# Scratch transfers issued by GpSimd, more staging buffers, and modulation sums closed later, in a two-layer hybrid diffusion backbone

## The chip, the cores and the metric

The kernel runs on one core of a Trainium2 chip. A core has a matrix engine (TensorE, PE), a vector engine (VectorE, DVE), a scalar engine (ScalarE, ACT), GpSimd (POOL) and a sync engine (SyncE, SP). Each works through its own list of instructions in order and waits on semaphores where it needs another engine or a transfer. A transfer is issued by an instruction in one of these lists, and is carried out by the 16 DMA engines that the issuers share. The metric is the device time of one execution in microseconds (us); lower is better.

## The reference

One latent sequence of 256 tokens (a grid of 4 rows of 64) and 256 context tokens, model width 2048, two layers, all float32. Layer 0 has a mixer of eight bidirectional gated-DeltaNet heads (GDN) beside eight neighbourhood-attention heads (NA), layer 1 a short gated convolution; each is followed by a SwiGLU feed-forward of hidden width 5632. Every layer is modulated by six vectors computed from the conditioning vector. Cut to what matters here:

```
for l in range(DEPTH):
    sh1, sc1, g1, sh2, sc2, g2 = jnp.split(jax.nn.silu(c) @ ada_w[l] + ada_b[l], 6, axis=-1)
    h = modulate(x_lat, norm_mix[l], sh1, sc1)          # rmsnorm(x, g) * (1 + scale) + shift
    ...
# even mixer, h latent and hc context
ka, va, kb, vb, a, b, qa, qb, za = split_segments(h @ w_in, EVEN_SEGS)   # hc: the first six
ka, va, qa = short_conv_silu([ka, va, qa], conv_w)
o_l = gdn_bidirectional(q_l, k_l, va, g, beta, s_ctx_fin)   # chunks of 64, both directions
y_gdn = rmsnorm(o_l, gdn_norm) * silu(za)
# attention: window keys of the grid plus all context keys in one softmax
s_loc = q @ k_window * scale + bias_from(rpb);  s_ctx = q @ k_ctx * scale
y_na = softmax(concat(s_loc, s_ctx)) @ concat(v_window, v_ctx)
y = concat(y_gdn, y_na) @ w_out
# GDN, per chunk: T = inverse(I + strictly_lower(beta * k k^T * decay)), then a scan over chunks
```

## The kernel before, in words

**Projections.** Every large product is done as three matmuls: weights and activations are each split into a high and a low part (whi, wlo and so on). A weight tile raw (128x1024, 512 KB) is loaded by SP; ACT copies it to whi (L169), DVE subtracts to get wlo (L238), PE runs hi by hi, lo by hi and hi by lo into PSUM (L284, L285, L287, and L293 to L295 in the last step, and L309 to L313 where the output has features on the partitions). An evacuation function then empties each PSUM tile mm.

**The even mixer**, some 200 to 900 us into the span, is a chain of such streams over column blocks of the input projection: keys KA and values VA of GDN, gates, queries QA, then QB, KB, VB of the attention heads and the gate ZA, then the output projection. The evacuations of QB, KB and VB (`stage`) copy a PSUM tile into a staging tile nst (two buffers), by turns on ACT (L164) and DVE (L166), and store it to DRAM scratch qb_d, kb_d, vb_d (L1051, issued by ACT). ZA uses the same tiles for its store to zd.

**Beside the streams** runs the GDN work. Keys and values go through DRAM scratch too: kd, vd_ and qTd are stored when a head's projection is done; `chunk_matrices` reloads ktok (L776), transposes it to kT and stores that (kTd, L795); it builds the strictly lower blocks n64, n32, stores them (nd64, nd32) and brings the 32x32 diagonal blocks through DRAM (dl, L825, back as lsol) into a layout in which POOL's memset and DVE's 31 steps solve all of them at once (zsol). The result goes out as dz (L846), and `inverses` reloads n64, n32 and the blocks (xd<-dz, xdT<-dz) and completes the inverse with small matmuls (Y, L887). Then scan steps (L927 to L960) run, one chunk after the other. Each reload waits for its store.

**Neighbourhood attention** (`na_scores`, `na_values`) runs head by head: load kb, qb, the relative bias br (one buffer, two issues of ACT at L1081), bq = br + band mask (DVE, L1084), scores (L1088, L1089), softmax, transposes (L188), reload of vb and the values (L1112).

**The modulation sums** (`ada_job`) stream the 512x or 1024-wide blocks of the modulation weights (araw) in 16 steps through DVE, acc = acc + araw * c (L332), into an acc that POOL zeroed (L327) and into whose first row SP loaded the bias (L328). A block then closes: PE sums over partitions (L338). A `Pump` takes such steps at a rate among the steps of the streams.

**What sets the order.** The program is handed to a scheduler that lays out every engine's list by its own simulated times. So an edit at one place can move instructions everywhere. Where two instructions of one engine compete, the list decides, and an instruction that waits holds everything behind it in its list.

**Counters of transfers.** A transfer signals one of a few counters. Those issued by SP and ACT share eight of them, listed as DMAHW0 to DMAHW7 in the engines' lists below; those issued by POOL have others, DMASW0 to DMASW7. An issue that takes a counter waits until the transfer that had it before is through.

Of the kernel before, what the change touches and what calls it, by code (L numbers as in the profile page):

```python
# [41 lines left out]
NPT = 1  # L42
AB = 3
# [4 lines left out]
NST = 2  # L48
# [57 lines left out]
def body(tc, x, c, ctx, c_ctx, ada_w, ada_b, norm_mix, norm_ffn, ffn_w_gate, ffn_w_up, ffn_w_down,  # L106
# [212 lines left out]

    def ada_job(pool_, l, seg, kind, gamma=None, width=1024, bufs=2):  # L320

        wr = ada_w[l].rearrange("(k p) n -> p k n", p=128)
        nf = width // 128
        for blk in range(D // width):
            c0 = seg * D + blk * width
            acc = pool_.tile([128, width], F32, name="acc", tag="acc", bufs=1)
            POOL.memset(acc, 0.0)  # L327
            SP.dma_start(acc[0:1, :], ada_b[l:l + 1, c0:c0 + width])  # L328
            for k in range(KT):
                raw = pool_.tile([128, width], F32, name="araw", tag="araw", bufs=bufs)  # L330
                SP.dma_start(raw, wr[:, k, c0:c0 + width])
                DVE.scalar_tensor_tensor(acc, raw, cT[:, k:k + 1], acc, op0=OP.mult, op1=OP.add)  # L332
                yield
            fs_ = slice(blk * nf, (blk + 1) * nf)
            p = smt()
            if width < 1024:
                for f in range(nf):
                    PE.matmul(p[:, f:f + 1], acc[:, f * 128:(f + 1) * 128], ones[:, 0:1], start=True, stop=True)  # L338
                pc = p
            else:  # L340
                ah = pool_.tile([128, width], F32R, name="ah", tag="ah", bufs=1)
                al = pool_.tile([128, width], F32R, name="al", tag="al", bufs=1)
                split(ah, al, acc, DVE)
                for f in range(nf):
                    for a in (ah, al):
                        PE.matmul(p[0:nf, 0:128], pick[:, nf - 1 - f:2 * nf - 1 - f], a[:, f * 128:(f + 1) * 128],
                                  start=f == 0 and a is ah, stop=f == nf - 1 and a is al)
                g = pool_.tile([16, 128], F32, name="grow", tag="grow", bufs=1)[0:nf]
                acopy(g, p[0:nf, 0:128])
                if kind == "row":  # L350
                    ACT.dma_start(row_d[l, seg][fs_], g)
                    continue
# [6 lines left out]
        if kind == "row" and width < 1024:  # L359
            p = smt()  # L360
            transpose(p[0:16, 0:128], gcol[l, seg])
            g = pool_.tile([16, 128], F32, name="grow", tag="grow", bufs=1)
            DVE.tensor_copy(g, p[0:16, 0:128])
            SP.dma_start(row_d[l, seg], g)
# [7 lines left out]
    class Pump:  # L372
        def __init__(self, jobs, steps, total):
            self.it = (s for j in jobs for s in j)
            self.rate = total / max(steps, 1)
            self.due = 0.0
            self.done = False
# [246 lines left out]
    def ka_evac(q):  # L624
        def done(kt, ss):
            normalise(kt, 4, rstd(kvp, ss, [128, 4, 4], 16, 1.0, "rk"))
            ACT.dma_start(hslice(kd, 0, 4, q), kt.rearrange("p t h e -> p t (h e)"))
        return head_evac(4, q, 0, done, True)

    def va_evac(q):  # L630
        def done(vt, ss):
            ACT.dma_start(hslice(vd_, 0, 4, q), vt.rearrange("p t h e -> p t (h e)"))
        return head_evac(4, q, 8, done, False)

    def qa_evac(q):
        def done(qt, ss):
# [3 lines left out]
            for g in range(2):  # L640
# [6 lines left out]
                ACT.dma_start(qTd[:, q * 4 + g * 2:q * 4 + g * 2 + 2, :], qf)  # L647
# [126 lines left out]
    def load_tok(tag, d_, t0, q):  # L774
        t = g4(tag, tag).rearrange("p (t h e) -> p t h e", t=2, h=4)
        SP.dma_start(t.rearrange("p t h e -> p t (h e)"), hslice(d_, t0, 2, q))  # L776
        return t

    def load_feat(tag, src, pool_=None, bufs=1):
        t = (pool_ or gw).tile([128, 1024], F32, name=tag, tag=tag, bufs=bufs).rearrange("p (h t) -> p h t", h=4)  # L780
        SP.dma_start(t, src)
        return t

    def chunk_matrices(seq):
# [6 lines left out]
        for q in range(2):  # L791
# [3 lines left out]
            SP.dma_start(kTd[:, seq, q * 4:q * 4 + 4, :], kT)  # L795
# [26 lines left out]
        ACT.dma_start(nd64, n64)  # L822
        ACT.dma_start(nd32, n32)
# [19 lines left out]
        for d in range(2):  # L843
            for v in range(2):
                src = (zsol, lsol)[d ^ v][d * 64:(d + 1) * 64].rearrange("p r c -> p (r c)")
                (SP, ACT)[v].dma_start(dz[v, :, :, d].rearrange("b q t e -> (b q) t e"), src)  # L846
        return nd64, nd32, dz

    def inverses(parts, q):
# [4 lines left out]
        SP.dma_start(n64, nd64[:, q * 8:q * 8 + 8, :])  # L854
        SP.dma_start(n32, nd32[:, q * 8:q * 8 + 8, :])
# [187 lines left out]
    def stage(dst, n, by=None):  # L1043

        def f(i, *p):
# [5 lines left out]
            ACT.dma_start(dst(i), st_)  # L1051
# [21 lines left out]
    def na_scores(h):  # L1073
        kb = nap.tile([128, 512], F32, name="kb", tag="kb", bufs=2)
        qb = nap.tile([128, 256], F32, name="qb", tag="qb", bufs=2)
        bq = nap.tile([128, 6, 64], F32, name="bq", tag="bq", bufs=2)
        br = nap.tile([128, 6, 64], F32, name="br", tag="br", bufs=1)
        for half in range(2):
            src = bass.AP(tensor=ev_rpb.tensor, offset=ev_rpb.offset + h * 465 + (5 - half) * 31 + 15 - 63,
                          ap=[[1, 64], [31, 6], [1, 64]])  # L1080
            ACT.dma_start(br[half * 64:half * 64 + 64], src)  # L1081
        SP.dma_start(kb, kb_d[:, h, :])
        SP.dma_start(qb, qb_d[:, h, :])
        DVE.tensor_tensor(bq, br, bandf[:, None, :].to_broadcast([128, 6, 64]), op=OP.add)  # L1084
# [16 lines left out]
    def na_values(h, ss):  # L1101
        vb = nap.tile([128, 4, 128], F32, name="vb", tag="vb", bufs=2)
# [13 lines left out]
    def za_evac(ti, n, p):  # L1116
# [4 lines left out]
        ACT.dma_start(zd[:, ti, n * 512:(n + 1) * 512], o)  # L1121
# [282 lines left out]
```

## Time and profile before

| | |
|---|---|
| median of 3 timed runs | 2842.87 us (2839.62 to 2844.02) |
| the profiled execution, its own time | 2848.17 us |
| its span | 2846.4 us |
| PE busy | 2732.5 us (96%) |
| DVE, ACT, POOL busy | 1924.8 (68%), 1308.3 (46%), 51.1 us (2%) |
| DMA queues | SP's 652.48 MB, ACT's 25.73 MB; none of POOL's |

A row of a view of groups gives the line, the engine, the operation, the tile written and those read, the shape, the count, the busy time, the mean of one in ns, and the idle time of the engine just before with what ended it ("<- DVE nst L166": released by DVE's instruction on nst at line 166). A row of the waits gives the total, the count and the longest. A row of the timeline gives the start, the duration, and in brackets the idle time before it. PEclk is the clock granted to PE as a share of full speed.

### The profile page before, as it was taken

Reading aid. Unit: us, or ns where it says so; the run is one execution under the profiler, and the core shown is the slowest. Engines: PE = TensorE matmul, PEld = TensorE weight load, DVE = VectorE, ACT = ScalarE, POOL = GpSimd, SP = SyncE. Lnnn points to the kernel's source line nnn. Section 1 sums busy time; section 2 is a strip of 40 time slices with the busy share of each in tenths; the row PEclk is TensorE's granted clock in tenths of the full one; section 3 lists DMA queues with packets and bytes.
Section 4 is the critical chain, followed back from the end, with each engine's and each line's share of the span. In section 5 each row is a group of like instructions: output and inputs, shape, how many; then the busy total and the mean of one; then the engine's idle time right before and its main releaser. Section 6 shows DMA issues by size and latency. Waiting matters only on the chain.

```text
span 2846.4 us, 40363 instructions
## 1 busy us (share of the span) xinstructions
PE 2732.5 (96%) x15113; PEld 2281.6 (80%) x15113; DVE 1924.8 (68%) x2647; ACT 1308.3 (46%) x1945; POOL 51.1 (2%) x77
## 2 busy tenths in 40 slices
PE   5999999989989999999999999999999999999998
PEld 3699989888767778888888878878878888888886
DVE  3387767857667878776677768897678644445665
ACT  3267543222354544444445545444454444444554
POOL 0000001000000000000000000000000000000000
PEclk9999999999999999999999999999999999999999
DMA  9955568777758599987788657998559766656653
GB/s 345 311 177 164 143 208 253 243 225 236 210 170 278 200 318 346 347 285 249 272 305 282 198 175 243 328 319 306 179 179 332 262 188 180 195 186 215 192 192 126
DMA packets 284927, 680.78 MB, mean 239 GB/s; under 512 B 57273, under 2 KB 97313, under 8 KB 283323
## 3 DMA queue, kind: packets, MB, share of 16 engines
q1 hardware_dynamic: 262148, 652.48, 69.4%
q10 hardware_dynamic: 22583, 25.73, 3.0%
q8 instruction: 118, 1.93, 0.3%
q14 instruction: 78, 0.64, 0.1%
HBM read 657.63 MB, written 20.48 MB: 238 GB/s over the span
## 4 chain that ended last, share of the span: by engine, by line
PE 70%; DMA 15%; DVE 9%; issue 3%; ACT 2%; SPq 1%; POOL 0%; ACTq 0%; DVEq 0%; POOLq 0%
PE mm L287 17%; PE mm L285 17%; PE mm L284 17%; DMA araw<-in_ada_w_dram 11%; PE mm L313 7%; DVE acc L332 3%; DVE wlo L238 3%; PE sm L188 2%; PE mm L293 2%; PE mm L295 2%; PE mm L294 2%; DMA raw<-in_od_w_in_dram 1%; DMA acc<-in_ada_b_dram 1%; PE gd L477 1%; ACT whi L169 0%
## 5 line engine op out<-in xcount | busy, mean ns | idle before, releaser
L238 DVE TENSOR_TENSOR wlo<-raw,whi 128x1024 fp32r<-128x1024 f32 x800 | 971.5, 1222 | 452.3 <-ACT whi L169 446.3
L169 ACT ACTIVATE whi<-raw 128x1024 fp32r<-128x1024 f32 x800 | 841.9, 1058 | 875.5 <-PE mm L287 632.4
L332 DVE SCALAR_TENSOR_TENSOR acc<-araw,cT,acc 128x1024 f32<-128x1024 f32 (+1 forms) x416 | 431.2, 1037 | 228.4 <-DMA araw<-in_ada_w_dram 198.8
L285 PE MATMUL mm<-wlo,fhi 128*128 128x512 f32 x1232 | 473.6, 394 | 0.2 <-DVE wlo L238 0.2
L284 PE MATMUL mm<-whi,fhi 128*128 128x512 f32 x1232 | 470.9, 396 | 0.6 <-ACT fhi L1187 0.6
L287 PE MATMUL mm<-whi,flo 128*128 128x512 f32 x1232 | 392.2, 392 | 0.1
L284 PEld LDWEIGHTS mm<-whi,fhi 128*128 128x128 f32 x1232 | 232.4, 189 | 50.4 <-ACT fhi L1187 1.0
L287 PEld LDWEIGHTS mm<-whi,flo 128*128 128x128 f32 x1232 | 231.0, 188 | 50.7 <-DVE flo L1189 0.3
L285 PEld LDWEIGHTS mm<-wlo,fhi 128*128 128x128 f32 x1232 | 232.5, 189 | 48.7 <-DVE wlo L238 0.7
L284 PE MATMUL mm<-whi,ahi 128*128 128x512 f32 x672 | 259.8, 392 | 0.0
L285 PE MATMUL mm<-wlo,ahi 128*128 128x512 f32 x672 | 259.4, 391 | 0.0
L287 PE MATMUL mm<-whi,alo 128*128 128x512 f32 x672 | 209.7, 392 | 0.0
L313 PE MATMUL mm<-hllo,whi 128*128 128x256 f32 x640 | 181.1, 287 | 0.0
L313 PE MATMUL mm<-hlhi,wlo 128*128 128x256 f32 x600 | 169.4, 288 | 2.0 <-issue 1.5
L313 PE MATMUL mm<-hlhi,whi 128*128 128x256 f32 x600 | 167.5, 290 | 1.0 <-DVE hlhi L502 1.0
L172 ACT ACTIVATE ahi<-prodT 128x256 fp32r<-128x256 f32 x176 | 73.0, 417 | 194.7 <-PE mm L285 187.6
L285 PEld LDWEIGHTS mm<-wlo,ahi 128*128 128x128 f32 x672 | 126.2, 188 | 27.5
L284 PEld LDWEIGHTS mm<-whi,ahi 128*128 128x128 f32 x672 | 126.2, 188 | 27.2
L287 PEld LDWEIGHTS mm<-whi,alo 128*128 128x128 f32 x672 | 126.1, 188 | 27.3
L285 PE MATMUL mm<-wlo,dhi 128*128 128x512 f32 x336 | 127.3, 398 | 2.6 <-DVE wlo L238 2.4
L313 PEld LDWEIGHTS mm<-hllo,whi 128*128 128x128 f32 x640 | 124.0, 194 | 0.4
L284 PE MATMUL mm<-whi,dhi 128*128 128x512 f32 x336 | 123.5, 396 | 0.3 <-DVE u_t L1329 0.3
(399 smaller groups left out, 4055.9 us busy)
## 6 DMA issues: line engine op xcount, KB each, us to landing
araw<-in_ada_w_dram SPq DMA_DIRECT2D x288, 512.0 KB
raw<-in_ffn_w_down_dram SPq DMA_DIRECT2D x176, 512.0 KB
raw<-in_ffn_w_gate_dram SPq DMA_DIRECT2D x160, 512.0 KB
raw<-in_ffn_w_up_dram SPq DMA_DIRECT2D x160, 512.0 KB
raw<-in_ev_w_in_dram SPq DMA_DIRECT2D x112, 512.0 KB
araw<-in_ada_w_dram SPq DMA_DIRECT2D x192, 256.0 KB
raw<-in_od_w_in_dram SPq DMA_DIRECT2D x96, 512.0 KB
raw<-in_ev_w_out_dram SPq DMA_DIRECT2D x32, 512.0 KB
```

The lines of the kernel that those rows point to most:

```text
L169: ACT.activation(dst, src, AF.Copy)
L172: ACT.activation(hi, src, AF.Copy)
L188: return PE.transpose(dst, src, ident[:n, :n])
L238: DVE.tensor_tensor(lo, raw, hi, op=OP.subtract)
L284: PE.matmul(ps[ti][n], a, hi[:, n * 512:(n + 1) * 512], start=first, stop=False)
L285: PE.matmul(ps[ti][n], a, lo[:, n * 512:(n + 1) * 512], start=False, stop=False)
L287: PE.matmul(ps[ti][n], b, hi[:, n * 512:(n + 1) * 512], start=False, stop=False)
L293: PE.matmul(ps[ti][n], lh(t), hi[:, c_], start=False, stop=False)
L294: PE.matmul(ps[ti][n], lh(t), lo[:, c_], start=False, stop=False)
L295: PE.matmul(ps[ti][n], ll(t), hi[:, c_], start=False, stop=hi is group[-1][0])
L313: PE.matmul(ps[f][:, n * 256:(n + 1) * 256], wt, mv(w, k), start=False, stop=i == len(ks) - 1 and g == len(group) - 1 and j == 2 and w == ...
L332: DVE.scalar_tensor_tensor(acc, raw, cT[:, k:k + 1], acc, op0=OP.mult, op1=OP.add)
```

## The change

Three things change, and two of them through the tile sizes of the same code.

1. POOL issues 86 transfers that ACT or SP issued: the stores kd, vd_, qTd, kTd, nd64, nd32, dl, dz, zd and the 24 of the staging tile, and the reloads of ktok, vtok, kT, qT, n64 and n32. The reloads of lsol that ACT issued go to SP; xd<-dz and xdT<-dz stay with SP.
2. The staging tile gets 4 buffers in place of 2 (NST), vb 3 in place of 2. The tile br is gone: SP loads the bias straight into bq (3 buffers in place of 2), and the mask is added in place.
3. In the modulation sums the first step writes acc without reading it (no memset), the bias is loaded as a small tile of its own and added at the closing (by one more small matmul for blocks 512 wide, by DVE in place of ACT's copy for those 1024 wide), blocks 512 wide have two acc, and they close three steps into the next block (LAG).

```
-NST = 2
+NST = 4
+LAG = 3
...
     def ada_job(pool_, l, seg, kind, gamma=None, width=1024, bufs=2):
-            acc = pool_.tile([128, width], F32, name="acc", tag="acc", bufs=1)
-            POOL.memset(acc, 0.0)
-            SP.dma_start(acc[0:1, :], ada_b[l:l + 1, c0:c0 + width])
-            for k in range(KT):
-                ...
-                DVE.scalar_tensor_tensor(acc, raw, cT[:, k:k + 1], acc, op0=OP.mult, op1=OP.add)
-                yield
+        def close(blk, acc, bias):
+            if width < 1024:
+                PE.matmul(p[:, 0:nf], bias, ident[0:nf, 0:nf], start=True, stop=False)
                 for f in range(nf):
-                    PE.matmul(p[:, f:f + 1], acc[:, f * 128:(f + 1) * 128], ones[:, 0:1], start=True, stop=True)
+                    PE.matmul(p[:, f:f + 1], acc[:, f * 128:(f + 1) * 128], ones[:, 0:1], start=False, stop=f == nf - 1)
             else:
                 ...
-                acopy(g, p[0:nf, 0:128])
+                DVE.tensor_tensor(g, p[0:nf, 0:128], bias, op=OP.add)
+        for blk in range(nblk):
+            acc = pool_.tile([128, width], F32, name="acc", tag="acc", bufs=1 if width == 1024 else 2)
+            bias = pool_.tile([16, 128], F32, name="abias", tag="abias", bufs=1 if width == 1024 else 2)[0:nf]
+            SP.dma_start(bias, ada_b[l, c0:c0 + width].rearrange("(f p) -> f p", p=128))
+            for k in range(KT):
+                ...
+                if k:
+                    DVE.scalar_tensor_tensor(acc, raw, col, acc, op0=OP.mult, op1=OP.add)
+                else:
+                    DVE.tensor_scalar(acc, raw, col, None, op0=OP.mult)
+                if k == LAG and closing:
+                    closing.pop()()
+                yield
+            if width == 1024:
+                close(blk, acc, bias)
+            else:
+                closing.append(lambda a=(blk, acc, bias): close(*a))
...
     def load_tok(tag, d_, t0, q):
-        SP.dma_start(t.rearrange("p t h e -> p t (h e)"), hslice(d_, t0, 2, q))
+        POOL.dma_start(t.rearrange("p t h e -> p t (h e)"), hslice(d_, t0, 2, q))
...
-        SP.dma_start(dl.rearrange("b r n c -> (b r) n c"), dgs)
+        POOL.dma_start(dl.rearrange("b r n c -> (b r) n c"), dgs)
-                (SP, ACT)[d].dma_start(lsol[p0:p0 + 16], dl[b, :, d * 16:(d + 1) * 16, :].rearrange("r n c -> n r c"))
+                SP.dma_start(lsol[p0:p0 + 16], dl[b, :, d * 16:(d + 1) * 16, :].rearrange("r n c -> n r c"))
...
-                (SP, ACT)[v].dma_start(dz[v, :, :, d].rearrange("b q t e -> (b q) t e"), src)
+                POOL.dma_start(dz[v, :, :, d].rearrange("b q t e -> (b q) t e"), src)
-        SP.dma_start(n64, nd64[:, q * 8:q * 8 + 8, :])
+        POOL.dma_start(n64, nd64[:, q * 8:q * 8 + 8, :])
...
     def stage(dst, n, by=None):
-            ACT.dma_start(dst(i), st_)
+            POOL.dma_start(dst(i), st_)
...
     def na_scores(h):
-        bq = nap.tile([128, 6, 64], F32, name="bq", tag="bq", bufs=2)
-        br = nap.tile([128, 6, 64], F32, name="br", tag="br", bufs=1)
+        bq = nap.tile([128, 6, 64], F32, name="bq", tag="bq", bufs=3)
-            ACT.dma_start(br[half * 64:half * 64 + 64], src)
+            SP.dma_start(bq[half * 64:half * 64 + 64], src)
-        DVE.tensor_tensor(bq, br, bandf[:, None, :].to_broadcast([128, 6, 64]), op=OP.add)
+        DVE.tensor_tensor(bq, bq, bandf[:, None, :].to_broadcast([128, 6, 64]), op=OP.add)
...
     def na_values(h, ss):
-        vb = nap.tile([128, 4, 128], F32, name="vb", tag="vb", bufs=2)
+        vb = nap.tile([128, 4, 128], F32, name="vb", tag="vb", bufs=3)
```

The lines of the changed kernel stand 26 or 27 further down: L1051 before is L1078 after, L1112 is L1138, L960 is L987, and helpers move by one (L164 to L165, L169 to L170, L188 to L189).

From the feed-forward on (some 945 us into the span) PE's order is nearly the same. In the mixer it is not. Three places:

ACT at the end of the first VB stream, before. Names in brackets are the counters waited for: an engine's own, or those of transfers.

```order
L1051 DMA vb_d<-nst 128x512 [waits DMAHW2_49,Activation_49]
L1051 DMA vb_d<-nst 128x512 [waits DMAHW5_49,DVE_49]
L942 ACTIVATE vd<-gd,brest 128x128 [waits PE_49]
L942 ACTIVATE vd<-gd,brest 128x128 x3
L169 ACTIVATE whi<-raw 128x1024 [waits DMAHW7_49,PE_49]
L164 ACTIVATE nst<-mm 128x512 [waits DMAHW2_49]
L1051 DMA vb_d<-nst 128x512 [waits DMAHW4_49,Activation_49]
L169 ACTIVATE Y<-gd 128x256 [waits PE_49]
L1051 DMA vb_d<-nst 128x512 [waits DMAHW2_49,DVE_49]
```

The same stores after, now in POOL's list:

```order
L886 MEMSET xdT 128x2048 [waits DMAHW6_49,DMAHW5_49,PE_49]
L803 DMA ktok<-kd 128x2x512 [waits DMASW2_49,PE_49]
L1078 DMA vb_d<-nst 128x512 [waits Activation_49]
L1078 DMA vb_d<-nst 128x512 [waits DMASW4_49,Activation_49]
L1078 DMA vb_d<-nst 128x512 [waits DMASW5_49,DVE_49]
L1078 DMA vb_d<-nst 128x512 [waits DMASW6_49,DVE_49]
L873 DMA dz<-zsol 8x8x1024 [waits DMASW7_49,DVE_49,Pool_49]
L873 DMA dz<-zsol 8x8x1024 [waits DMASW0_49]
```

Before, each store in ACT's list waits for a DMAHW counter, and vd, whi, the next nst and Y stand behind it. After, the stores wait for POOL's counters, and stand in POOL's list behind a memset of xdT and a reload of ktok that wait for PE.

SP at the start of the attention heads, after:

```order
L1107 DMA bq<-in_ev_rpb_dram 64x6x64 [waits PE_49]
L1107 DMA bq<-in_ev_rpb_dram 64x6x64
L1108 DMA kb<-kb_d 128x512
L1109 DMA qb<-qb_d 128x256 [waits DMAHW2_49]
L1107 DMA bq<-in_ev_rpb_dram 64x6x64
L1107 DMA bq<-in_ev_rpb_dram 64x6x64 [waits DMAHW4_49]
L1108 DMA kb<-kb_d 128x512 [waits DMAHW5_49]
L1109 DMA qb<-qb_d 128x256 [waits DMAHW6_49]
```

The loads of the bias, which stood in ACT's list (L1081), now stand ahead of kb and qb in SP's, and the first of them waits for PE.

PE at the end of the mixer, before:

```order
L927 MATMUL gd<-state,qT 128x128 x4
L938 MATMUL gd<-R,xdT 128x128 x4
L1112 MATMUL sm<-PT,vb 128x256 x4
L1088 MATMUL sm<-kb,qb 128x512
L1089 MATMUL sm<-bq,cs 128x256
L960 MATMUL gd<-vn,AT 128x128 x4
L1088 MATMUL gd<-kb,qb 128x512
L1089 MATMUL gd<-bq,cs 128x256
L1088 MATMUL sm<-kb,qb 128x512
L1089 MATMUL sm<-bq,cs 128x256
L284 MATMUL mm<-whi,yhi 128x512 x4
```

and after:

```order
L285 MATMUL mm<-whi,yhi 128x512
L286 MATMUL mm<-wlo,yhi 128x512
L288 MATMUL mm<-whi,ylo 128x512 x2
L954 MATMUL gd<-state,qT 128x128 x4
L965 MATMUL gd<-R,xdT 128x128 x4
L189 MATMUL sm<-cs,s 128x128 x4
L987 MATMUL gd<-vn,AT 128x128 x4
L1114 MATMUL gd<-kb,qb 128x512
L1115 MATMUL gd<-bq,cs 128x256
```

The last matmul of the scan (L960, now L987) stood before the first matmul of the output projection (mm<-whi,yhi), and now stands after 48 of them.

More of the change, by code (lines that the diff above doesn't have):

```diff
@@ L317, in fm_stream @@
             yield
+    closing = []
     def ada_job(pool_, l, seg, kind, gamma=None, width=1024, bufs=2):
@@ L323, in ada_job @@
         nf = width // 128
[L324 to L333 removed]
+        nblk = D // width
+        def close(blk, acc, bias):
             fs_ = slice(blk * nf, (blk + 1) * nf)
@@ L631, in done @@
         def done(vt, ss):
-            ACT.dma_start(hslice(vd_, 0, 4, q), vt.rearrange("p t h e -> p t (h e)"))
+            POOL.dma_start(hslice(vd_, 0, 4, q), vt.rearrange("p t h e -> p t (h e)"))
         return head_evac(4, q, 8, done, False)
@@ L1120, in za_evac @@
         DVE.tensor_tensor(ov, ov, gnb[:, None, :].to_broadcast([128, 4, 128]), op=OP.mult)
-        ACT.dma_start(zd[:, ti, n * 512:(n + 1) * 512], o)
+        POOL.dma_start(zd[:, ti, n * 512:(n + 1) * 512], o)
     held = na_scores(0)
```

41 lines of the change are left out of this document (26 added, 15 removed).

## The prediction

> **What bounds the kernel now.** I read the page first.
>
> ```profile
> span 2846.4 us, 40363 instructions
> PE 2732.5 (96%) x15113; PEld 2281.6 (80%) x15113; DVE 1924.8 (68%) x2647; ACT 1308.3 (46%) x1945; POOL 51.1 (2%) x77
> ```
>
> TensorE (PE) is busy for 96% of the span, so an edit that adds no TensorE work can gain only from the 114 us in which PE stands still and from what those stops bring with them. The edit lies almost wholly in the even layer's mixer, so the next view is a table of stretches (columns: span of the stretch, busy us of PE, PE weight load, DVE, ACT, POOL, granted PE clock, DMA share, GB/s).
>
> ```profile
> 300.00:500.00 200.00, 189.65 (x1968) 185.30 (x1967) 144.84 (x269) 89.76 (x157) 15.08 (x26) 0.98 0.71 213
> 500.00:600.00 100.00, 87.85 (x727) 77.03 (x727) 70.03 (x151) 23.88 (x48) 7.12 (x7) 0.93 0.79 245
> 700.00:800.00 100.00, 92.98 (x486) 76.23 (x485) 61.83 (x122) 38.58 (x85) 0.00 (x0) 0.97 0.64 182
> 1200.00:1500.00 300.00, 300.00 (x1380) 245.84 (x1379) 208.63 (x193) 133.04 (x150) 2.87 (x3) 1.00 0.81 280
> ```
>
> In the feed-forward stretch PE has no idle time at all: nothing the edit does there can gain. In the mixer 12.2 us of 500 to 600 and 7.0 us of 700 to 800 are idle, and the granted clock is below 1. DMA is at 64 to 79%, not full. The view of PE's waits names what it stood for (total us, times, longest).
>
> ```profile
> PE mm L309 <- DVE nst L166: 5.1, 1, 5.1
> ...
> PE gd L887 <- ACT Y L169: 3.8, 1, 3.8
> ...
> PE mm L284 <- ACT whi L169: 3.8, 2, 3.5
> PE sm L1089 <- DVE bq L1084: 3.4, 1, 3.4
> ...
> PE sm L338 <- DVE acc L332: 2.0, 1, 2.0
> ```
>
> These five lie at 570.4, 582.3, 717.1, 735.5 and 506.4 us: together 5.1 + 3.8 + 3.5 + 3.4 + 2.0 = 17.8 us, nearly all the idle time of the two stretches. Each names an object that the edit touches. The same table over short windows around the five shows a second price.
>
> ```profile
> 505.00:515.00 10.00, 8.02 (x39) 6.61 (x39) 8.53 (x22) 3.29 (x7) 0.53 (x1) 0.83 0.77 246
> 569.00:579.00 10.00, 4.90 (x66) 4.36 (x67) 4.30 (x5) 2.57 (x6) 0.00 (x0) 0.83 0.73 167
> 580.00:592.00 12.00, 8.16 (x166) 7.79 (x165) 5.83 (x13) 2.94 (x6) 0.00 (x0) 0.72 0.91 280
> 716.00:726.00 10.00, 6.38 (x19) 4.36 (x18) 6.03 (x13) 2.95 (x3) 0.00 (x0) 0.83 0.92 267
> 734.00:744.00 10.00, 6.60 (x22) 4.16 (x22) 4.71 (x11) 1.06 (x1) 0.00 (x0) 0.83 0.86 266
> ```
>
> After every one of these stops the clock granted to PE drops for a few us. The lost clock is (1 - 0.83) x 10 = 1.7 us four times and (1 - 0.72) x 12 = 3.4 us once: 10.2 us. The five stops cost 17.8 + 10.2 = 28.0 us in all.
>
> Why they happen is told by ScalarE's (ACT's) row of events; rows marked ACTq are issues of transfers.
>
> ```profile
> 564.58 0.60 ACT L164 ACTIVATE nst<-mm 128x512 f32<-128x512 f32 x1 [0.25 <-PE mm L295]
> 573.66 2.11 ACTq L1051 DMA_DIRECT2D vb_d<-nst  x2
> ...
> 585.29 0.38 ACTq L1051 DMA_DIRECT2D vb_d<-nst  x1
> 585.72 0.38 ACT L169 ACTIVATE Y<-gd 128x256 f32<-128x256 f32 x1 [7.32 <-DMA araw<-in_ada_w_dram]
> ...
> 712.37 2.35 ACTq L1081 DMA_DIRECT2D br<-in_ev_rpb_dram  x2
> 719.12 0.32 ACTq L1051 DMA_DIRECT2D vb_d<-nst  x1
> 719.49 2.95 ACT L169 ACTIVATE whi<-raw 128x1024 fp32r<-128x1024 f32 x3 [8.49 <-DMA br<-in_ev_rpb_dram]
> ```
>
> At 565.2 ACT has filled the staging tile nst and should issue its store; the issue comes at 573.66, 8.5 us later. The two nst tiles are then both taken, DVE's copy into nst waits, PSUM is not emptied, and PE stops at 570.4. At 585.29 and 719.12 it is the same again: a PE producer (Y, whi) stands in ACT's order behind a store that has not been issued. The waits say the same: ACT waits for transfers it never reads.
>
> ```profile
> ACT whi L169 <- DMA araw<-in_ada_w_dram: 25.8, 6, 7.7
> ```
>
> ACT's whi is made from raw, not from araw. What it stood for is a store ahead of it: the order of ACT lists, for each store, a counter that transfers of SP also use (at 565 it is the one of SP's xd<-dz). A store on ACT thus waits until an earlier transfer of SP has landed, with all ACT work behind it.
>
> **The change, part by part.** *The stores and reloads go to GpSimd (POOL): 86 issues, 44 of them from ACT, the rest from SP.* The issue itself is cheap where it is now:
>
> ```profile
> L1051 ACTq DMA_DIRECT2D vb_d<-nst x8: 321/326/375, 573.7 to 719.1; - x8
> ```
>
> so 44 x 0.33 = 14 us of ACT's time is not the point (ACT is 46% busy); the wait in front is. In the changed order ACT's copies and splits have no store between them, and POOL's stores use counters of their own. With four nst tiles, 8.5 us of delay of a store no longer reaches PE: 128x512 evictions come in pairs. So I take the stops at 570, 582 and 717 as gone: 5.1 + 3.8 + 3.5 + (1.7 + 3.4 + 1.7) = 19.2 us.
>
> *br goes.* The stop at 735.5 is this chain:
>
> ```profile
> 738.31 0.56 DVE L1084 TENSOR_TENSOR bq<-br,cs 128x384 f32<-128x384 f32 x1 [6.48 <-DMA br<-in_ev_rpb_dram]
> ```
>
> There was one br tile for every head, loaded by ACT; now the bias goes into one of three bq tiles, issued by SP. Gone: 3.4 + 1.7 = 5.1 us.
>
> *The modulation sums.* Twenty-six POOL memsets go, and the first of 16 DVE steps a block is a plain multiply:
>
> ```profile
> L327 POOL MEMSET acc<- 128x1024 f32 x14 | 13.4, 956 | 1084.6 <-DVE al L173 803.0 <-PE sm L188 223.5 <-ACT fhi L1187 58.1
> ...
> L859 POOL MEMSET xdT<- 128x2048 f32 x4 | 7.2, 1812 | 149.0 <-PE gd L477 133.4 <-PE gd L938 15.7
> ```
> ```profile
> L332 DVE SCALAR_TENSOR_TENSOR acc<-araw,cT,acc 128x1024 f32<-128x1024 f32 x224 | 287.4, 1283 | 133.8 <-DMA araw<-in_ada_w_dram 124.1 <-DMA acc<-in_ada_b_dram 6.0 <-issue 0.9
> ...
> L516 DVE TENSOR_SCALAR xn<-xn,n0r 128x2048 f32<-128x2048 f32 x4 | 4.9, 1283 | 0.0
> ```
>
> L516 does 2048 columns in the time that L332 does 1024, so the 14 wide first steps fall to about half: 14 x 0.64 = 9 us of DVE, and less for the 12 narrow ones. DVE is 68% busy and PE is full wherever it runs, so I cost this at nothing; it would show only where PE waits for DVE. The memsets are counted at nothing too, POOL being 2% busy. What PE does see is the closing of a block three steps later, when the sum is long done: 2.0 + 1.7 = 3.7 us at 506.4. Each narrow closing gets one more small matmul:
>
> ```profile
> 508.40 0.83 PE L338 MATMUL sm<-cs,acc 128*128 128x1 f32 x6 [1.99 <-DVE acc L332]
> ```
>
> 0.83 / 6 = 0.14 us, 12 times: 1.7 us.
>
> *What POOL charges.* No transfer is issued by POOL in this trace, so I bound it. Where a transfer stands on a path that PE waits for, the reload of ktok (4) and of n (4), the round trips dl (2) and dz (2), a dearer issue is a later start: 12 places. Below: POOL issues as ACT does, 0.33 us, extra 0; a gain below that is not to be had, since the data still take their time. Above: an issue costs POOL as much as its longest operation, 1.81 us (L859), extra 1.48, 17.8 us in sum. I take the 0.96 us of L327, an operation of POOL on all 128 partitions as these transfers are, extra 0.63: 12 x 0.63 = 7.6 us.
>
> *More buffers* cost nothing by themselves. *Order:* the scheduler lays out every engine anew; as a price for one new stop I count one clock loss of 1.7 us.
>
> Sum: gains 19.2 + 5.1 + 3.7 = 28.0; costs 1.7 + 7.6 + 1.7 = 11.0; net 17.0 us. Against the profiled execution (2848.2, of which 1.8 lie outside its span of 2846.4) that is 2831.2; the profiled one is 5.3 us above the median 2842.9, so in terms of the timed runs 2825.9.
>
> The likeliest case's own range: with POOL at its upper price 2842.9 - 28.0 + 1.7 + 17.8 + 1.7 = 2836.1; with no extra price, no new stop, and half of the 10.4 us idle in 300 to 500 and half of its clock loss (200 x 0.02 = 4) gone as well, 2842.9 - 28.0 + 1.7 - 5.2 - 2.0 = 2809.4.
>
> **Rivals.** *A, the gain is given back at the end of the mixer.* The recurrence (GDN) ends with a chain of scan steps. Before, its last matmul stands ahead of the output projection's first; in the changed order the recurrence comes two steps later, its last matmul after 48 matmuls of the output projection.
>
> ```profile
> 803.66 1.05 PE L960 MATMUL gd<-vn,AT 128*128 128x128 f32 x8
> ...
> 814.32 1.13 PE L960 MATMUL gd<-vn,AT 128*128 128x128 f32 x8 [1.68 <-DVE o_t L932]
> ...
> 854.19 1.97 PE L1112 MATMUL sm<-PT,vb 128*128 128x256 f32 x8
> ```
>
> A step takes 814.32 - 803.66 = 10.7 us, two are 21.3. Against it: the attention heads end 40 us later than the scan (854.19), so there is room for both; for it: every chain of this tail is serial. If nothing covers it, 2825.9 + 21.3 = 2847.2, no change or a little slower.
>
> *B, slower: POOL's transfers are late, not dear.* POOL works in order, so a reload behind a memset that waits, or a store that waits, is late by as much; and what POOL has to do for a transfer may take far longer than for SP. The place is the chain in which each link is a transfer (dl, lsol, dz, n, ktok); a link now lasts up to
>
> ```profile
> 307.54 4.09 DMA n<-nd
> ```
>
> If each of the 12 is late by one such time, 12 x 4.09 = 49.1, with a clock loss at six of them 10.2: 2842.9 - 28.0 + 1.7 + 59.3 = 2875.9. It decides from (28.0 - 1.7) / 12 = 2.2 us a transfer. For it: the changed order puts the ktok reload of the second sequence behind a memset of xdT that waits for PE. Against it: between dl and its use other work of PE runs, and only some links are bare. The Trainium skill ("SBUF — State Buffer", section "SBUF: two separate sides") has a rule that speaks for B: a transfer issued by GpSimd is starved of descriptors while DVE runs one of its double-rate operations, and it advises issuing from ACT or SP. Here such operations are short and few:
>
> ```profile
> L1097 DVE TENSOR_SCALAR s<-s,l 128x512 f32<-128x512 f32 x16 | 7.7, 483 | 0.5
> ```
>
> With the 12 narrow first steps that is 28 x 0.48 = 13.5 us in some 560 us of mixer, 2.4%, so the rule by itself adds at most 12 x 0.024 x 0.48 = 0.1 us to the sum. No run here shows the lock.
>
> *C, the stalls stay.* Then ACT's late stores were late since all transfers are, and the wait goes to other counters: with the bq of a head on SP behind a weight load, and its tile free only when the head before has been read, the stop at 735 stays, and those at 570 to 590 with it. Time 2842.9 + 1.7 = 2844.6. For it: SP's queue is the fullest. The Trainium skill ("DMA: Bandwidth & Descriptors", section "Issuing engines are not separate DMA queues") says this too: several issuing engines save only the sequencer's time to start a transfer. By that rule the gain is 44 x 0.33 us of ACT, hidden, so 2844.6. The trace differs: ACT stood 8.5 us for an issue of 0.33 us, and the copies behind it stood too; the rule counts the issue alone and not what waits behind it.
>
> **How the numbers follow.** Forecast 0.56; A 0.18; B 0.15; C 0.11. A measurement here can tell about 0.2%, 5.7 us, from no change. The forecast's own range, 2809 to 2836, is all faster. A splits, since some of the two steps will be covered: 0.06 faster, 0.08 same, 0.04 slower. C is 0.10 same and 0.01 faster; B slower, 0.15. Faster 0.63, same 0.18, slower 0.19. The predicted time is the likeliest's, 2826. The range for 8 in 10 reaches down to 2807 (2809 and the spread of the runs) and up past A and C to 2856, part of B; what remains of B is left out.
>
> **What would show it.** Right: no stop of over 1 us at the closings (L338), at nst, Y, whi and bq in 500 to 740; 500 to 600 with PE above 95 us and clock above 0.97; ACT no longer waiting for araw, br or dz. POOL's price: the time from issue to landing of ktok, n, dl, dz against SP's, and PE's waits at the users of ktok and xd. Rival A: L960 (now 27 lines further down) ending after the last attention head, with PE waiting there. Rival B: new PE stops of several us at the block inverses and at the transposes of ktok. Wrong altogether: if the stops go and the end of the mixer comes no earlier, or the layers after 945 us, where the order is the same, change.

## The result, and the profile after

| | before | after |
|---|---|---|
| median of 6 runs | 2843.44 us (2839.62 to 2846.58) | 2864.69 us (2859.44 to 2867.34) |
| ratio | | 1.0072, 95% interval 1.0059 to 1.0085 |
| profiled execution, span | 2848.17, 2846.4 us | 2865.56, 2863.8 us |

The change makes the kernel 0.7% slower, some 21 us. 2826 was predicted, with a range of 2807 to 2856.

The page after:

```profile
span 2863.8 us, 40416 instructions
PE 2739.5 (96%) x15137; PEld 2291.1 (80%) x15137; DVE 1917.8 (67%) x2661; ACT 1306.5 (46%) x1932; POOL 82.4 (3%) x137
```

Where the time went is read from a place that both kernels pass: the first transpose of the normalised rows that opens the first feed-forward (columns: nanoseconds of one, least, median and most; then the first and the last start). Before and after:

```profile
L188 PE MATMUL sm<-cs,xc x96: 270/326/476, 943.9 to 2111.3; 128*128 128x128 f32 x96
```
```profile
L189 PE MATMUL sm<-cs,xc x96: 270/300/476, 971.6 to 2128.7; 128*128 128x128 f32 x96
```

The mixer ends 971.6 - 943.9 = 27.7 us later. What follows is shorter: 2863.8 - 971.6 = 1892.2 against 2846.4 - 943.9 = 1902.5 us, 10.3 us. So in these two profiles there is a loss of 28 in the mixer and a gain of 10 where PE's order hardly differs.

The table by stretch, for the stretch that the prediction named (500 to 600) and its neighbours. After:

```profile
190.00:240.00 50.00, 50.00 (x425) 49.64 (x424) 44.26 (x85) 26.60 (x40) 2.88 (x5) 1.00 0.75 242
240.00:500.00 260.00, 238.53 (x2322) 232.49 (x2320) 183.54 (x363) 140.56 (x285) 34.65 (x62) 0.95 0.60 183
500.00:600.00 100.00, 97.47 (x633) 87.48 (x634) 82.08 (x183) 32.84 (x68) 22.14 (x35) 1.00 0.83 260
600.00:944.00 344.00, 309.79 (x2107) 258.68 (x2106) 210.58 (x364) 127.31 (x252) 17.85 (x28) 0.95 0.66 205
```

The same of the kernel before, without 500 to 600, which the prediction shows:

```profile
190.00:240.00 50.00, 50.00 (x428) 49.64 (x428) 41.33 (x92) 34.42 (x79) 2.93 (x6) 1.00 0.44 129
240.00:500.00 260.00, 245.18 (x2423) 239.41 (x2422) 190.64 (x377) 137.73 (x267) 19.68 (x35) 0.99 0.66 201
...
600.00:944.00 344.00, 321.65 (x1962) 268.08 (x1961) 235.93 (x399) 138.73 (x266) 2.64 (x5) 0.98 0.70 223
```

From 500 to 600 PE is busy for 97.5 us at full clock, against 87.9 at 0.93: just what the prediction asked for. But the idle time has moved. From 240 to 500 it is 21.5 us where it was 14.8, from 600 to 944 34.2 where it was 22.4, and the clock is 0.95 in both. And between 190 and 240 DMA moves 242 GB/s where it moved 129. PE's waits after name new objects:

```profile
PE gd L907 <- DMA xd<-dz: 7.8, 2, 6.7
PE gd L965 <- DVE R L948: 6.6, 4, 4.2
...
PE sm L1138 <- DVE PT L167: 4.5, 1, 4.5
...
PE mm L310 <- ACT nst L1077: 2.7, 1, 2.7
...
PE sm L334 <- DMA abias<-in_ada_b_dram: 2.2, 1, 2.2
```

The stops at nst (DVE), Y, whi, bq and acc of before are gone or under 1 us. In their place PE waits for the blocks that come back through dz, for R and PT that stand on DVE behind the mask addition to bq, for ACT's nst, and for the bias of a closing.

### The profile page after: what moved, and what is told of

Same layout as the page of the kernel before. It is cut to its first block, busy times and chain, and to the rows that moved or that the text cites. A ratio compares the mean times of both kernels' runs of the same rounds, so it can differ in the third digit from the quotient of the medians.

```text
span 2863.8 us, 40416 instructions
## 1 busy us (share of the span) xinstructions
PE 2739.5 (96%) x15137; PEld 2291.1 (80%) x15137; DVE 1917.8 (67%) x2661; ACT 1306.5 (46%) x1932; POOL 82.4 (3%) x137
## 4 chain that ended last, share of the span: by engine, by line
PE 75%; DMA 12%; DVE 6%; ACT 3%; issue 3%; SPq 1%; POOL 0%; DVEq 0%; POOLq 0%; ACTq 0%
PE mm L288 18%; PE mm L286 18%; PE mm L285 18%; DMA araw<-in_ada_w_dram 9%; PE mm L314 7%; DVE acc L374 2%; PE mm L296 2%; PE mm L294 2%; PE mm L295 2%; PE sm L189 2%; DMA bq<-in_ev_rpb_dram 2%; DVE wlo L239 1%; PE gd L504 1%; ACT whi L170 0%; PE sm L1138 0%
## 5 line engine op out<-in xcount | busy, mean ns | idle before, releaser
L170 ACT ACTIVATE whi<-raw 128x1024 fp32r<-128x1024 f32 x800 | 843.2, 1059 | 910.7 <-PE mm L288 635.3
L374 DVE SCALAR_TENSOR_TENSOR acc<-araw,cT,acc 128x1024 f32<-128x1024 f32 (+1 forms) x390 | 404.3, 1037 | 215.6 <-DMA araw<-in_ada_w_dram 210.7
```

The costliest lines, as they stand in the source:

```text
L170: ACT.activation(dst, src, AF.Copy)
L374: DVE.scalar_tensor_tensor(acc, raw, col, acc, op0=OP.mult, op1=OP.add)
```

## The experiments

Ratios are against the kernel before, run beside it on the same chip, with 95% intervals. First the two ideas that the trace of after suggested: each part has its own price (theory 1: POOL's transfers are late, SP's bias loads are late), or the new order as such is worse (theory 2).

**The bias loads undone.**

```
-            SP.dma_start(bq[half * 64:half * 64 + 64], src)
+            ACT.dma_start(br[half * 64:half * 64 + 64], src)
```

> The changed kernel with one part undone: the attention bias is loaded by ACT into one tile br and added into bq (2 buffers), as before. Theory 1 (each loss belongs to its part; SP's bias loads land 6.6 us after their issue and DVE's copies for PE stand behind the addition): the stops of 4.2 us at 781 and 4.5 us at 824 go with their 1.7 and 3.4 us of clock, 13.8 us in all, and the old stop at bq (3.4 + 1.7) may come back: 2864.7 - 13.8 = 2851 to 2856. Theory 2 (the loss lies in the new order as such, the scan two steps later and colliding with the last attention head): any rebuilt order gives a time of its own that the part does not explain; if the end of the mixer stays as it is, 2862 or more.

Measured 2848.8 us, 1.0026 (1.0014 to 1.0038). Some 13 us came back (0.46% of the time), about what theory 1 said. In the changed kernel this is what PE waited for (DVE, then PE):

```profile
783.55 0.56 DVE L1110 TENSOR_TENSOR bq<-bq,cs 128x384 f32<-128x384 f32 x1 [6.49 <-DMA bq<-in_ev_rpb_dram]
784.02 1.12 DVE L948 SCALAR_TENSOR_TENSOR R<-gd,negegc,vtok 128x128 f32<-128x128 f32 x4
```
```profile
785.20 1.20 PE L965 MATMUL gd<-R,xdT 128*128 128x128 f32 x8 [4.21 <-DVE R L948]
```

With the loads undone PE's longest wait for R is 1.5 us and for PT 0.8, and one for bq is back, 2.5 us.

**The GDN round trips undone**: kTd, nd, dl, lsol, dz and the reloads on SP and ACT as before, POOL with the stores alone.

```
-            POOL.dma_start(kTd[:, seq, q * 4:q * 4 + 4, :], kT)
+            SP.dma_start(kTd[:, seq, q * 4:q * 4 + 4, :], kT)
...
-                POOL.dma_start(dz[v, :, :, d].rearrange("b q t e -> (b q) t e"), src)
+                (SP, ACT)[v].dma_start(dz[v, :, :, d].rearrange("b q t e -> (b q) t e"), src)
```

> The changed kernel with the GDN round trips back on SP and ACT as before (kTd, nd, dl, lsol, dz, and the reloads of ktok, vtok, kT, qT, n); POOL issues only the stores kd, vd_, qTd, of the staging tile and zd. Theory 1 (POOL's transfers are late, 6.2 us from issue to landing for dz): the stop of 6.7 us before the block inverse at 602 goes with its 5.1 us of clock, 11.8 us: 2853; with the stops at nst and abias near 402 (4.9 + 5.1, where the store of vd_ waits for the counter of dz) up to 21.8: 2843. Theory 2: a time that the part does not explain, 2850 to 2880.

Measured 2852.65 us, 1.0035 (1.0024 to 1.0046): the sum of theory 1's first term. But the stop that it named is still there, 5.7 us at the block inverse, now with dz issued by SP and ACT. The number was right by luck; the reason was not, and what gave the time back stays open.

**POOL's transfers alone**, in the kernel before (the 86 issues and lsol, nothing else).

> The kernel before with POOL issuing the 86 transfers (and lsol by SP), nothing else: two staging tiles, br by ACT. The prediction's sum: ACT's stops at 570, 582 and 717 go (19.2), POOL's price 7.6: 2843.4 - 11.6 = 2832. Theory 1 (a POOL transfer lands 2 to 3 us later than SP's, 12 of them in chains): 2843.4 - 19.2 + 12 x 2.5 + some clock = 2854 or more, with the stop before xd. Theory 2: no rule, 2830 to 2870.

Measured 2842.55 us, 0.9999 (0.9987 to 1.0012). Neither the gain of 11.6 that the prediction worked out nor the loss of theory 1. A store of the staging tile costs POOL 0.55 us to issue where it cost ACT 0.33 (view of groups, changed kernel):

```profile
L1078 POOL DMA_DIRECT2D vb_d<-nst x8 | 4.4, 553 | 36.2 <-ACT nst L165 23.1 <-DVE nst L167 13.1
```

**The modulation sums alone**, in the kernel before.

> The kernel before with the modulation sums alone changed. Theory 1: the stops at 1040 (2.7 + 1.7) and 1904 (2.0 + 1.7, with wide blocks beside them) and those of the closings at 506 and 542 (2.0 + 0.9 + 1.7) go, 12.7 us, and one closing waits for its bias as at 402 of the changed kernel (2.2 + some clock): 2843.4 - 12.7 + 4 = 2835. Theory 2: the first 900 us are reordered, 2835 give or take 15.

Measured 2851.66 us, 1.0022 (1.0003 to 1.0041): a loss where theory 1 had a gain, and just outside the 15 us either way that theory 2 allowed.

**The bias loads alone**, in the kernel before.

> The kernel before with the bias loads alone changed (by SP straight into three bq, added in place). Theory 1: DVE's additions wait for SP's loads as in the changed kernel (8 waits, 26 us in sum, against 4 and 12 before) and PE's work behind them on DVE is late: 2842.7 + 8 to 15 = 2851 to 2858. Theory 2, or if the loss needed the whole change: 2842.7 give or take 5.

Measured 2845.04 us, 1.0013 (1.0003 to 1.0023): some 4 us, under half of what theory 1 gave them and within the 5 of theory 2.

**The changed kernel with the old sums.**

> The changed kernel with the modulation sums as before (memset, bias into the first row of acc, one acc, closed at the end of the block); POOL's transfers, the buffers and the bias loads by SP stay. Theory 1 (the losses add up by part: sums +9, bias loads on SP +15, POOL's transfers about 0 alone): 2864.7 - 9 to - 12 = 2854, and the scan ends again before the output projection begins. Theory 2 (each order is a draw of its own): a time anywhere in 2840 to 2865, with no relation to the other runs.

Measured 2850.46 us, 1.0029 (1.0016 to 1.0043): near the sum of theory 1.

**POOL's transfers with the buffers**, in the kernel before (four staging tiles, three vb).

> The kernel before with POOL's 86 transfers, four staging tiles and three vb, without the other two parts. Theory 1: as POOL alone (2842.6), and the stop of 2.0 + 3.4 us at nst that two staging tiles left there goes: 2837 to 2840. Theory 2: 2842.6 give or take 10.

Measured 2840.78 us, 0.9998 (0.9989 to 1.0008). The stop at nst did not go; the section on the prediction says why.

**The new sums without the delay**: each block closes at the end of its own steps, two accumulators.

```
-            if width == 1024:
-                close(blk, acc, bias)
-            else:
-                closing.append(lambda a=(blk, acc, bias): close(*a))
+            close(blk, acc, bias)
```

> The kernel before with the modulation sums changed but for the delay: each block is closed at the end of its own 16 steps. If the delayed closing is what makes the sums slower (closings pile up, a bias waits for the closing before), the loss of 9 us goes: 2842.7 - 0 to - 4 = 2839 to 2843. If it is the added matmul with the new order of the scan, it stays: 2850.

Measured 2862.17 us, 1.0068 (1.0047 to 1.0089). Without the delay the sums alone cost nearly as much as the whole change. So the delay is not the harm. Theory 3 came from a table of all these profiles: with a second accumulator the sums run ahead, and the GDN solves come late. The table has the start of the second dz store, which carries the result of the second GDN solve, and the end of the mixer.

| kernel | accumulators | second dz starts | mixer ends | rest of the span |
|---|---|---|---|---|
| before | 1 | 558.0 | 943.9 | 1902.5 |
| POOL alone | 1 | 555.4 | 939.9 | 1900.1 |
| bias loads alone | 1 | 563.3 | 946.3 | 1898.6 |
| POOL and buffers | 1 | 559.8 | 943.0 | 1900.3 |
| changed, old sums | 1 | 552.8 | 947.6 | 1902.2 |
| changed | 2 | 590.8 | 971.6 | 1892.2 |
| changed, bias loads undone | 2 | 588.1 | 956.9 | 1892.4 |
| changed, round trips undone | 2 | 586.8 | 955.9 | 1892.2 |
| new sums alone | 2 | 619.9 | 960.6 | 1892.3 |
| new sums, no delay | 2 | 614.2 | 973.6 | 1890.7 |

With one accumulator the second solve is out by 553 to 563 us and the mixer ends by 948. With two it is out at 587 to 620 and the mixer ends at 956 to 974. The nine profiles still to come keep the groups apart, with less room: seven with one accumulator have the store at up to 570 and the end at 942 to 951, two with two have 582 and 620, and 973 and 965. So the order is not a mere draw, as theory 2 had it. Why the ends within each group differ is not settled: one program profiled twice (the wide blocks alone, below) ended its mixer at 942.8 and at 949.5, and in the group of two the later solve does not go with the later end (619.9 with 960.6, 590.8 with 971.6). What the second accumulator does is seen in the instructions that touch acc, counted by stretch (DVE's busy time and count is the third figure). Before, and after:

```profile
0.00:310.00 310.00, 0.00 (x0) 0.00 (x0) 11.94 (x16) 0.00 (x0) 0.53 (x1) 0.99 0.75 239
310.00:600.00 290.00, 5.92 (x48) 5.93 (x48) 59.97 (x80) 0.00 (x0) 3.16 (x6) 0.96 0.73 224
```
```profile
0.00:310.00 310.00, 0.00 (x0) 0.00 (x0) 23.33 (x32) 0.00 (x0) 0.98 0.76 247
310.00:600.00 290.00, 6.49 (x48) 6.38 (x48) 61.31 (x84) 0.00 (x0) 0.97 0.72 222
```

With one accumulator the second block waits for the closing of the first, which comes at some 400 us: 16 steps are done ahead of the first solve. With two, 32 are, 11.4 us of DVE and 16 transfers of 256 KB more, right where GDN's keys are being prepared (the 242 GB/s of 190 to 240 us). The first dz store moves from 364.9 to 394.1 us. Both solves start late (first and last start of their operations, before and after):

```profile
L837 DVE TENSOR_TENSOR sub_tmp<-lsol,zsol x62: 181/359/424, 311.6 to 557.6; 128x31 f32<-128x31 f32 x4, 128x60 f32<-128x60 f32 x4, 128x87 f32<-128x87 f32 x4, 128x112 f32<-128x112 f32 x4
```
```profile
L864 DVE TENSOR_TENSOR sub_tmp<-lsol,zsol x62: 191/356/428, 331.3 to 589.8; 128x31 f32<-128x31 f32 x4, 128x60 f32<-128x60 f32 x4, 128x87 f32<-128x87 f32 x4, 128x112 f32<-128x112 f32 x4
```

The second solve begins at 498.2 before and at 532.1 after, with 58 and 83 steps of the sums ahead of it. It is not longer, 59.8 and 58.1 us, with 29 steps between its operations in both.

**One accumulator, no delay, new form**, in the kernel before; and the same in the changed kernel.

```
-            acc = pool_.tile([128, width], F32, name="acc", tag="acc", bufs=1 if width == 1024 else 2)
+            acc = pool_.tile([128, width], F32, name="acc", tag="acc", bufs=1)
```

> The kernel before with the new modulation sums, but one accumulator and no delay: a block is closed after its own 16 steps, and the next block's first step waits for that. Theory 3 (the second accumulator lets 32 steps run on DVE and SP ahead of the first GDN solve where 16 did, and the solve and all behind it in the mixer come later; the sums' new form is good after the mixer, where every kernel with it was about 8.5 us shorter): the mixer is as before, 2842 - 8.5 = 2833 to 2836. Rival (the matmul and the load of the bias, or the new form itself, cost in the mixer): 2850 to 2860 as in the two runs with two accumulators.

Measured 2840.01 us, 1.0005 (0.9995 to 1.0015). This kernel and the one without the delay, 1.0068, differ in this one buffer and in nothing else. The loss of the mixer is gone; the mixer ends at 946.6, and of the gain behind it (1889.9) nothing is left in the timed runs.

> The changed kernel with one accumulator for the narrow blocks and no delay; POOL's transfers, buffers, bias loads by SP and the form of the sums stay. Theory 3: as the changed kernel without its sums (2850) less the gain behind the mixer, 2842; 22 us less than the changed kernel. Rival (the changed kernel's loss is of POOL and SP's loads): 2860 or more.

Measured 2838.63 us, 0.9989 (0.9976 to 1.0001): 0.83%, some 24 us, under the changed kernel by one buffer and the place of the closing. The last start of a dz store of zsol, 566.6, and the mixer's end:

```profile
L870 POOL DMA_DIRECT2D dz<-zsol x4: 575/588/1198, 370.9 to 566.6; - x4
```
```profile
L189 PE MATMUL sm<-cs,xc x96: 270/273/474, 945.8 to 2104.2; 128*128 128x128 f32 x96
```

**The same with the bias loads by ACT**, as before the change:

> As the run before, but the attention bias loaded by ACT as before: POOL's transfers, four staging tiles, three vb, the new sums with one accumulator. Theory 3: 2841 (without the sums) - 8.5 = 2832, under both kernels. Rival: 2841 or more.

Measured 2842.81 us, 1.0000 (0.9984 to 1.0015): no loss, and the gain was missed.

**The second accumulator alone**, in the kernel before: memsets, bias and closings all as before.

```
-            acc = pool_.tile([128, width], F32, name="acc", tag="acc", bufs=1)
+            acc = pool_.tile([128, width], F32, name="acc", tag="acc", bufs=1 if width == 1024 else 2)
```

> The kernel before with one edit: two accumulators in place of one for the blocks 512 wide (memsets, bias in the first row, closing at the block's end all as before). Theory 3 (the second accumulator alone lets 32 steps run ahead of the first GDN solve in place of 16, and makes the mixer 16 to 28 us longer, as in the two kernels with two accumulators; without the new form there is no gain behind the mixer): 2841 + 16 to 28 = 2857 to 2869. Rival (it is the new form with its bias load and matmul, and two accumulators are harmless): 2841 give or take 5.

Measured 2857.86 us, 1.0057 (1.0041 to 1.0072): 16 us for one more buffer of 256 KB. The dz stores start at 400.7 and 619.5 us, and the mixer ends at 965.4:

```profile
L846 SPq DMA_DIRECT2D dz<-zsol x2: 611/654/698, 400.7 to 619.5; - x2
```
```profile
L188 PE MATMUL sm<-cs,xc x96: 270/273/473, 965.4 to 2124.7; 128*128 128x128 f32 x96
```

**No running ahead of the first solve**: the changed kernel, but its second narrow block uses the first one's accumulator; from then on two.

> The changed kernel, but the first narrow block closes at its end and the second uses the same accumulator, so that no more than 16 steps can run ahead of the first GDN solve; from the second block on there are two accumulators and the delay, as in the change. Theory 3a (the harm is the 16 extra steps between 190 and 240 us, which delay the first solve): it nearly all goes, 2840 to 2845. Theory 3b (any running ahead harms, the second solve too, with 64 steps ahead of it against 83 in the changed kernel and 58 before): 2845 to 2858.

Measured 2863.9 us, 1.0079 (1.0063 to 1.0095). Theory 3a falls, and the loss is above what theory 3b allowed too (2858). The first dz store is nearly on time (368.8 us), and the second is late by itself: the second solve takes 75.7 us where it took 59.8. The stretch of that solve, counting the instructions on acc alone, in this kernel and in the kernel before:

```profile
505.80:581.50 75.70, 2.16 (x16) 2.09 (x16) 30.43 (x42) 0.00 (x0) 1.00 0.80 260
```
```profile
498.20:558.00 59.80, 2.13 (x16) 2.02 (x16) 21.69 (x29) 0.00 (x0) 1.05 (x2) 0.97 0.76 246
```

The solve is 62 small operations on DVE, one after another; 42 steps of the sums now stand between them where 29 did, 8.7 us more of DVE. Summed over DVE's timeline, their waits for araw inside the solve are 10.9 us against 3.5. Together that is about the 15.9 us. So the steps ahead of the first solve are not needed for a late one: in the changed kernel the steps stand ahead of the solves, here inside the second. That a late solve is what makes the end of the mixer late (972.5 here) is argued and not shown. The kernel with one accumulator, no delay and the new form has 35 steps inside a second solve of 66.7 us, and its mixer still ends at 946.6.

**The wide blocks alone** in the new form, the narrow ones as before.

> The kernel before with the new sums only in the blocks 1024 wide (all behind the mixer but for the last), the blocks 512 wide as before. Theory 3: the gain behind the mixer alone, 2842 - 8.5 = 2833. Rival (that gain is luck of the order, or comes from the narrow blocks): 2842.

Measured 2838.22 us, 0.9987 (0.9975 to 0.9999), and measured once more:

> The new sums in the wide blocks alone, once more with more rounds. 0.9987 was measured, between 0.9975 and 0.9999. If the gain behind the mixer (about 8 us) is real: 0.997 to 0.999, clear of 1. If it was the order of one build's profile: 1.000.

2837.63 us, 0.9979 (0.9967 to 0.9991). A gain of some 4 to 6 us is there in the timed runs, where the profiles show 8 to 9 less behind the mixer than the kernel before. The profiles do not tie it to the new form: the kernel with the second accumulator alone has the old form, and its rest of the span is 2860.2 - 965.4 = 1894.8 us too.

**The changed kernel with one accumulator, again**:

> The changed kernel with one accumulator and no delay, once more with more rounds, to tell whether it is faster than the kernel before: 0.9989 was measured, between 0.9976 and 1.0001. If the gain behind the mixer (8 us) is kept and the mixer is 4 to 5 us longer than before, 0.9985 to 0.999; if not, 1.000.

2838.78 us, 0.9991 (0.9978 to 1.0004): not told apart from the kernel before. **POOL, buffers, and the new form in the wide blocks**:

> The new sums in the wide blocks, and POOL's 86 transfers with four staging tiles and three vb (the sums of the narrow blocks and the bias loads as before). POOL's part was 0.9998 and 0.9999 by itself: if the parts that do no harm add up, 0.997 to 0.999, as the wide sums alone; if POOL's late transfers begin to matter, above 1.000.

Measured 2834.47 us, 0.9970 (0.9957 to 0.9983). This beats both kernels: some 8.5 us under the kernel before, 29 under the changed one (0.0030 and 0.0102 of the time before).

```profile
span 2832.8 us, 40391 instructions
```

## Why the prediction was wrong

**The step that failed** is that more buffers "cost nothing by themselves", with the modulation sums counted at nothing but for their closings. That step looked at what a buffer does to the one who waits for it. It did not ask what the freed work runs into. The second accumulator alone costs 0.57%, and 0.63 points in the pair that has the new form without the delay (1.0068 and 1.0005). Three more pairs, in which the delay changes with it, have 0.17, 0.26 and 0.83 points, so the sign holds and the size depends on the rest. Without the second accumulator and the delay the whole change is 0.9989 and 0.9991. The kernel before had a cover that the prediction did not look at: the wait of the second block for the first one's closing kept 11.4 us of DVE work from running ahead of the first solve. So the second accumulator accounts for the loss. By what path is shown in part: the second solve is late in all seven profiles with two accumulators, and that the mixer ends late for this reason is argued. Why most of the predicted net gain of 17 us is missing without it too is told next.

**The stop at 570 was read wrongly.** It was put down to two full staging tiles behind ACT's late store. DVE's own events at that place, in the kernel before:

```profile
570.54 0.75 DVE L332 SCALAR_TENSOR_TENSOR acc<-araw,cT,acc 128x512 f32<-128x512 f32 x1 [5.50 <-DMA araw<-in_ada_w_dram]
572.93 0.75 DVE L332 SCALAR_TENSOR_TENSOR acc<-araw,cT,acc 128x512 f32<-128x512 f32 x1 [1.64 <-DMA araw<-in_ada_w_dram]
573.60 1.22 DVE L238 TENSOR_TENSOR wlo<-raw,whi 128x1024 fp32r<-128x1024 f32 x1
574.73 0.68 DVE L166 COPY nst<-mm 128x512 f32<-128x512 f32 x1
```

DVE did not wait for a tile. Its copy stood behind two steps of the sums that waited for araw. With four tiles and POOL's stores, in the kernel with POOL and buffers, it is the same:

```profile
581.64 1.54 DVE L332 SCALAR_TENSOR_TENSOR acc<-araw,cT,acc 128x512 f32<-128x512 f32 x2 [7.09 <-DMA araw<-in_ada_w_dram]
583.10 0.68 DVE L166 COPY nst<-mm 128x512 f32<-128x512 f32 x1
```

and PE waits 3.9 us for it. ACT's late issue was real, and here it was not what ended last. With POOL's transfers alone a stop of 2.0 us is left at Y (582) and one of 2.0 at nst, and in place of the one at 717 came one of 4.7 us for wlo at 712. So of the 12.4 us of stops in the 19.2 us of gain 8.7 are there again, and PE waits 5.0 us for o_t at the end of the scan (L960) where it waited 1.7.

**The gain of the closings** (3.7) was given back: in the changed kernel no closing waits for acc any more, but one waits for its bias (2.2 us), PE waits 2.7 us for ACT's nst just behind it, and from 400 to 415 us the granted clock is 0.66, 15 x 0.34 = 5.1 us.

**POOL's price** was put at 0.96 us an issue; for most of them it is 0.55, so the term of 7.6 was too high, and the time of B, 2875.9, finds no support in POOL alone. But with the gain behind ACT also mostly absent, the sum of the two, -11.6, came out as 0. Rival C had a time near this, 2844.6, though not all stops stayed where they were. The Trainium skill ("DMA: Bandwidth & Descriptors", section "Issuing engines are not separate DMA queues") states that issuing from several engines saves only the time to start a transfer. The 0.9999 for POOL alone agrees with it.

**DVE's first steps** were worked out as 9 us of DVE and counted at nothing for PE. With the new form in the wide blocks alone the timed runs are 4 to 6 us shorter, so nothing was too low. Whether the shorter steps do it, the closings of the wide blocks, or the order that the edit brings is not shown.

**br.** The stop of 3.4 us at bq went, but the wait stayed on DVE: 26.4 us in 8 waits where it was 11.9 in 4. This part of rival C was right; how much it costs depends on the rest (+0.13%, +0.31% and +0.46% in three pairs of kernels with and without it, -0.1% in a fourth), and that stays open.

**Rival A** held in part: the scan ends later and meets the last attention head, with stops of 3.5 and 3.0 us near 870 us; in this kernel the solves ahead of it are late too. **Rival B** had the sign, with 2875.9 where 2864.7 was measured, by a mechanism that POOL alone (0.9999) denies. What the prediction named as a sign of being right, PE above 95 us from 500 to 600 at full clock, came true in a kernel that is slower: a stretch with no idle time only says that the idle time is elsewhere.

## What to carry to other kernels

Before adding a buffer, ask what the work that it frees will run beside: where a scheduler lays out one order for an engine, an off-path stream that runs ahead can push back a serial chain on the same engine (here the 62 small operations of a solve), and a wait that looks idle may be what protects the chain. Read a stop on the engine that PE names, event by event, before going on to the next engine: the copy that is late may stand behind its own neighbour. And judge a change by where a common later event falls, not by one stretch, in more than one profile: here one program's mixer ended 6.7 us apart in two.

## What was not expected of the hardware

The issue of a staging store takes 0.55 us on POOL against 0.33 on ACT, and 86 transfers issued by POOL in place of SP and ACT made no difference that can be measured (0.9999, 0.9987 to 1.0012), round trips through DRAM included.
